# Four projections of a hybrid encoder block in seven block products of eight

## The chip, the core and the metric

The kernel runs on one core of a Trainium2 chip. The metric is the device time of one execution in microseconds (us): of three runs of the kernel before, 1034.06 to 1035.69 us, median 1035.56 us. The engines are named as in the profile: PE (TensorE, matrix products), DVE (VectorE), ACT (ScalarE), POOL (GpSimd) and SP (SyncE, which starts most DMAs).

## What is computed

One layer of a streaming encoder on 512 positions and 16 learned ones ahead of them, with model width 1024 and 2816 in the feed-forward. All is float32.

```python
u  = rmsnorm(h);  proj = u @ w_in                      # 1024 x 10256
y_conf = silu(layernorm(conv31(val * sigmoid(gate)))) @ w_conf_out
o      = chunk_gated_delta_rule(q, k, v, g, beta)      # 8 heads, sequential over chunks
y_dn   = (rmsnorm(o) * silu(z)) @ w_dn_out
h  = h + (g_conf * y_conf + g_dn * y_dn) @ w_out
up = conv3(rmsnorm(h) @ w_up)                          # 1024 x 5632
h  = h + (silu(up_gate) * up_val) @ w_down
out = rmsnorm(h)                                       # without the 16 learned positions
```

## The kernel before, in words

Activations lie transposed, features on the 128 partitions and positions along the row; a projection of 1024 features is eight tiles. Each weight tile (128 outputs x 1024 inputs, 512 KB) is one DMA into a buffer `wr` (three of them); `weights` (line 504) splits it into two parts in a rounded float32 form, `wh` by a cast on ACT and `wl` by a subtraction on DVE (two buffers of each). Activations are split in the same way by `split` (line 528): `oh`/`ol` for the delta rule's output, `ch`/`cl` for the convolution's, `mh`/`ml` for their gated sum, `hh`/`hl` for the second norm's input, `fh`/`fl` for the feed-forward.

`gemm` (line 515) makes one output tile: 8 input tiles, for each the three products low x high, high x high and high x low, each in two column halves of 258 to 260: 48 matmuls into one two-bank tile `p2` (two of them in PSUM). The eight output tiles of `w_dn_out` ('y'), of `w_conf_out` ('c', whose accumulators are named y too) and of `w_out` ('wo') follow the heads, then the 44 tiles of `w_up` ('up') and the 8 of `w_down` ('dn').

`up` (line 1207) multiplies the raw accumulator by the second norm's factor `r2` in two DVE instructions, so that PE can start on `w_up` before that factor is known; then three taps follow (ACT, and two DVE instructions `uy`), silu, the product with the other half, and the split into `fh`/`fl`.

In `grow` (line 893) the blocks of the heads' triangular inverses are put together by small matmuls (`gP`, `gX`); ahead of them, line 908 copies 32 blocks of 32x32x4 from `DU` into the tiles `Mn` (named mn) on ACT.

The order on each engine is made at build time: `Plan.order` (line 318) lists the instructions by priority, with prices of its own and offsets (`BIAS`, `LNP`, `UP` and others) by part of the program. On the chip each engine then works its list off in that fixed order, waiting at each instruction until what it needs is there.

```python
for i, (k, w, a) in enumerate(runs):
    for b, (c0, c1, *at) in enumerate(ranges):
        p0 = at[0] if at else 0
        PE.matmul(acc[:, b, p0:p0 + c1 - c0], lhsT=w[:, k * P:(k + 1) * P], rhs=a[k0 + k][:, c0:c1], ...)
```

Of the kernel before, what the change touches and what calls it, by code (L numbers as in the profile page):

```python
# [19 lines left out]
P = 128  # L20
# [16 lines left out]
ROW = T + PAD  # L37

# [104 lines left out]
RATE = 0.4453  # L143
# [37 lines left out]
GATES = [[12], [13], [15], [9], [0, 2], [], [7, 14, 8], [10, 1, 5, 3, 4, 6, 11]]  # L181

# [45 lines left out]
class Plan:  # L228
# [10 lines left out]
    def at(self, by, late=True):  # L239
# [3 lines left out]
        self.prio, self.late = self.prio + by, was or late and by > 0  # L243
# [3 lines left out]
    def add(self, eng, fn, a, k):  # L247
# [38 lines left out]
        o.tail = 950 + (2800 if fn == "dma_start" and o.lat > 700 and self.run(k) <= P else 0)  # L286
# [8 lines left out]
    def price(self, eng, fn, a, k, out):  # L295
# [10 lines left out]
        if fn == "dma_start":  # L306
            return 475, int(np.prod(out.shape)) * 4 / 290.0 * (1 if self.run(k) >= P else 2)
# [10 lines left out]
    def order(self):  # L318
# [70 lines left out]
        while len(out) < len(ops):  # L389
# [72 lines left out]
def record(A, out):  # L462
# [52 lines left out]
    def gemm(acc, ws, ah, al, ranges, k0=0, kn=None, first=True, last=True):  # L515
# [275 lines left out]
    def decays(h):  # L791
# [54 lines left out]

    ivt = {}
# [503 lines left out]
```

## Time and profile before

| | us |
|---|---|
| median of three runs | 1035.56 |
| the profiled execution | 1031.66 |
| its span, first to last instruction | 1029.9 |
| PE busy | 1015.1 |
| DVE busy | 717.1 |
| ACT busy | 473.6 |
| POOL busy | 9.4 |

The profile is one execution; its span leaves out some 1.8 us around it, and the execution itself is 3.9 us under the median. An engine's busy time is the time in which at least one of its instructions runs; idle time of an engine that nothing waits for costs nothing. Granted clock (PEclk) 1.00 is TensorE's upper level, 2.4 GHz.

### The profile page before, as it was taken

To read this page: it belongs to the slowest core of one execution; us is meant where nothing else is said; L and a number is where in the kernel's file an instruction comes from. 1 tells how busy PE (TensorE), PEld (TensorE's weight loads), DVE (VectorE), ACT (ScalarE), POOL (GpSimd) and SP (SyncE) were. 2 spreads that over 40 slices of the span, in tenths; PEclk is the share of its full clock that TensorE was granted. 3 is DMA by queue.
4 is the path that set the end of the run, shared out by engine and by line. 5 is a ranking of instruction groups with operands and counts; after the bars stand their busy time and mean duration, and the time that the engine had idled before them with its cause. 6 is when DMAs were issued, how large, how long until landed. Compare 5 with 4: busy or idle time off the path is not lost.

```text
span 1029.9 us, 20012 instructions
## 1 busy us (share of the span) xinstructions
PE 1015.1 (99%) x8430; PEld 973.8 (95%) x8430; DVE 717.1 (70%) x1237; ACT 473.6 (46%) x844; POOL 9.4 (1%) x45
## 2 busy tenths in 40 slices
PE   9998999999999999999999999999999999999996
PEld 7998999998999999999999999999999999988886
DVE  5987999999999999443565555666676767622334
ACT  6777713468545545444373334544434443422222
POOL 0000000000000000000000000000000000000000
PEclk9999999998999999999999999999999999999999
DMA  6243423241212133123214333222232222233332
GB/s 229 76 115 82 128 90 114 83 103 64 73 63 82 53 114 115 62 73 114 93 43 154 128 109 100 85 83 100 86 99 88 86 99 87 93 93 92 97 92 82
DMA packets 44042, 98.40 MB, mean 96 GB/s; under 512 B 12720, under 2 KB 19248, under 8 KB 43952
## 3 DMA queue, kind: packets, MB, share of 16 engines
q1 hardware_dynamic: 43952, 97.12, 29.5%
q8 instruction: 66, 1.08, 0.4%
q14 instruction: 24, 0.20, 0.1%
HBM read 93.89 MB, written 3.21 MB: 94 GB/s over the span
## 4 chain that ended last, share of the span: by engine, by line
PE 93%; DVE 4%; ACT 1%; DMA 1%; issue 0%; SPq 0%; DVEq 0%; ACTq 0%
PE up L459 25%; PE dn L459 12%; PE ga L459 9%; PE y L459 9%; PE q L459 5%; PE v L459 5%; PE z L459 5%; PE wo L459 5%; PE cv L459 4%; PE cg L459 4%; PE o L459 2%; DVE cv L459 1%; PE k L459 1%; PE rs L459 1%; PE S L459 1%; PE qk L459 1%
## 5 line engine op out<-in xcount | busy, mean ns | idle before, releaser
L459 DVE TENSOR_TENSOR wl<-wr,wh 128x1024 fp32r<-128x1024 f32 x157 | 189.2, 1206 | 154.3 <-PE dn L459 59.8
L459 ACT CAST wh<-wr 128x1024 fp32r<-128x1024 f32 x157 | 162.2, 1035 | 257.1 <-PE dn L459 58.2
L459 DVE SCALAR_TENSOR_TENSOR ca<-c,par,ca 128x516 f32<-128x516 f32 (+12 forms) x240 | 176.7, 745 | 3.7 <-ACT ca L459 1.0
L459 PE MATMUL up<-hl,wh 128*128 128x258 f32 x704 | 141.5, 282 | 0.0
L459 PE MATMUL up<-hh,wh 128*128 128x258 f32 x704 | 141.5, 282 | 0.0
L459 PEld LDWEIGHTS up<-hh,wh 128*128 128x128 f32 x704 | 109.2, 190 | 0.2 <-issue 0.2
L459 PEld LDWEIGHTS up<-hl,wh 128*128 128x128 f32 x704 | 108.7, 189 | 0.0
L459 PE MATMUL up<-hh,wl 128*128 128x258 f32 x704 | 92.3, 284 | 0.0
L459 PEld LDWEIGHTS up<-hh,wl 128*128 128x128 f32 x704 | 88.2, 190 | 0.0
L459 PE MATMUL dn<-fh,wh 128*128 128x512 f32 (+1 forms) x198 | 71.6, 370 | 0.0
L459 PE MATMUL dn<-fl,wh 128*128 128x512 f32 (+1 forms) x198 | 71.6, 370 | 0.0
L459 DVE SCALAR_TENSOR_TENSOR uy<-up,par,uy 128x512 f32<-128x512 f32 x88 | 65.9, 749 | 2.8 <-ACT uy L459 1.3
L459 DVE TENSOR_TENSOR up<-up,r 128x258 f32<-128x258 f32 x88 | 33.5, 420 | 47.4 <-PE up L459 44.6
L459 ACT ACTIVATE uy<-up,par 128x512 f32<-128x512 f32 x44 | 35.9, 817 | 55.8 <-DVE up L459 55.8
L459 PE MATMUL ga<-ul,wh 128*128 128x258 f32 (+1 forms) x256 | 58.0, 288 | 0.0
L459 PE MATMUL ga<-uh,wh 128*128 128x258 f32 (+1 forms) x256 | 57.2, 288 | 0.0
L459 DVE SCALAR_TENSOR_TENSOR cv<-ra,par,cv 128x528 f32<-128x528 f32 x69 | 51.7, 765 | 1.4 <-ACT cv L459 1.3
L459 PE MATMUL dn<-fh,wl 128*128 128x512 f32 (+1 forms) x198 | 45.4, 369 | 0.0
L459 PEld LDWEIGHTS dn<-fh,wh 128*128 128x128 f32 x198 | 37.2, 188 | 7.0
L459 PEld LDWEIGHTS dn<-fl,wh 128*128 128x128 f32 x198 | 37.2, 188 | 6.9
L459 PE MATMUL ga<-uh,wl 128*128 128x258 f32 (+1 forms) x256 | 43.1, 286 | 0.0
L459 PEld LDWEIGHTS ga<-ul,wh 128*128 128x128 f32 x256 | 42.2, 190 | 0.6 <-issue 0.4
(284 smaller groups left out, 2194.6 us busy)
## 6 DMA issues: line engine op xcount, KB each, us to landing
wr<-in_win SPq DMA_DIRECT2D x64, 512.0 KB, 3.4
wr<-in_wup SPq DMA_DIRECT2D x44, 512.0 KB, 3.4
wr<-in_wd SPq DMA_DIRECT2D x17, 512.0 KB, 3.5
wr<-in_wdn SPq DMA_DIRECT2D x8, 512.0 KB, 3.5
wr<-in_wco SPq DMA_DIRECT2D x8, 512.0 KB
wr<-in_wo SPq DMA_DIRECT2D x8, 512.0 KB, 3.4
wr<-in_wd SPq DMA_DIRECT2D x8, 384.0 KB, 3.5
x<-in_xT SPq DMA_DIRECT2D x8, 264.0 KB, 5.6
```

The lines of the kernel that those rows point to most:

```text
L459: getattr(engines[o.eng], o.fn)(*(get(x) for x in o.a), **{n: get(x) for n, x in o.k.items()})
```

## The change

Of the four projections of 'y', 'c', 'wo' and 'up', two output tiles (256 features) are made together, and two halves of the positions (258 each): a 2 x 2 block product, done in seven block products in the place of eight (`seven`). Each block product is 12 matmuls of 258 columns. The seven go by turns into two accumulators, each a one-bank tile of its own (`sx`, `sz`; four such tiles in all): three sums of weights and four of activations stand in for the operands, and partial results are read from an accumulator between two products that add up in it.

The sums of weights are made in DRAM, by accumulating DMAs that POOL starts (`presums`: five for a pair of tiles, 31 pairs; two pairs are under way at a time). The sums of activations are made by `factors` (four DVE instructions of 258 columns, four casts on ACT, four subtractions on DVE for a pair of tiles). `quarters` puts the results together in SBUF. The first three feed-forward tiles with their partners (`NPRE`, six of 44) stay as they were; for the rest the second norm's factor is multiplied into the activations ahead of the product. Residual tiles are written to DRAM and read back (`d_h`, `hr`). The copies of line 908 go from ACT to POOL. The planner's prices and offsets are new.

```diff
-BIAS = {'k3': -850, 'iv': -1500, 'd0': 150, ...
+BIAS = {'tp': 2330, 'h0': 400, 'h2': 240, ...
+NPRE = 3
+    def presums(src, n, hold):
+        r = [plan.tile("dram", "con", [P, 4, HD], F32, "ws") for _ in range(n)]
+        for m in range(n):
+          with plan.at(1):
+            h = {hold} | ({softs[-2]} if len(softs) > 1 else set())
+            plan.after = set(h)
+            G.dma_start(out=r[m][:, 0:2], in_=src[:, m, 0:3:2])
+            plan.after = set(h)
+            G.dma_start(out=r[m][:, 2:4], in_=src[:, m, 0:2])
+            G.dma_start(out=r[m][:, 1:3], in_=src[:, m, 3:4].broadcast_to([P, 2, HD]), accum_op=ALU.add)
+            G.dma_start(out=r[m][:, 0], in_=r[m][:, 1], accum_op=ALU.add)
+            G.dma_start(out=r[m][:, 3], in_=r[m][:, 0], accum_op=ALU.add)
+            softs.append(len(plan.ops) - 1)
+    def seven(src, m, sums, B, w, use):
+        X, Z = p1("sx")[:, :w], p1("sz")[:, :w]
+        tiles = (flat(src[:, m, 0:2]), flat(sums[m][:, 0:2]), flat(sums[m][:, 2:4]), src[:, m, 2])
+        for i, (b, to, first, what) in enumerate((('b11', X, True, 'p1'), ('b21', Z, True, 'c11b'),
+                                                  ('t2', X, False, 'u2'), ('t1', Z, True, 'c22b'),
+                                                  ('t3', X, False, 'u3'), ('b22', Z, False, 'c12b'),
+                                                  ('t4', X, False, 'c21'))):
+            if i % 2 == 0:
+                hi, lo = weights(tiles[i // 2], D if i < 6 else HD)
+            ...
+                PE.matmul(to, lhsT=x[:, c + k * P:c + (k + 1) * P], rhs=B[k][b][y], ...)
+            use(what, to)
+    def quarters(src, m, sums, B, w, n):
+            if what in ('p1', 'u2'):
+                S.copy(out=q(i, j), in_=acc)
+            elif what in ('c22b', 'c21'):
+                S.mul(out=q(i, j), in_=acc, mul=-1.0)
+            else:
+                V.tensor_tensor(out=q(i, j), in0=q(i, j), in1=acc, op=ALU.subtract if i else ALU.add)
...
-                S.copy(out=Mn[h][r, :, r], in_=D8(h)[r])
+                G.tensor_copy(out=Mn[h][r, :, r], in_=D8(h)[r])
...
+            g, v = quarters(A['wuq'], t - NPRE, wus, ub, 258, "up")
...
-            V.tensor_tensor(out=uv[:, b], in0=acc[:, b, :258], in1=r2v[b], op=ALU.mult)
```

The order on DVE in the feed-forward, before: two tiles (one pair). `wl` is the low part of a weight tile, the first `up` rows read accumulators, `uy` are taps, `fl` is the low part of the result.

```order
L459 TENSOR_TENSOR up_23_8660<-up_20_8588,r2_1_8033 128x258 x2
L459 TENSOR_TENSOR wl_101_8668<-wr_101_8484,wh_101_8634 128x1024
L459 SCALAR_TENSOR_TENSOR uy_11_8672<-up_23_8660,par_1_82,uy_11_8672 128x512 x2
L459 TENSOR_TENSOR up_25_8720<-up_22_8655,r2_1_8033 128x258 x2
L459 TENSOR_TENSOR wl_102_8729<-wr_102_8554,wh_102_8705 128x1024
L459 SCALAR_TENSOR_TENSOR uy_12_8732<-up_25_8720,par_1_82,uy_12_8732 128x512 x2
L459 TENSOR_TENSOR uy_11_8672<-uy_11_8672,uy_12_8732 128x512
L459 TENSOR_TENSOR fl_6_8782<-uy_11_8672,fh_6_8774 128x512
L459 TENSOR_TENSOR up_27_8790<-up_24_8718,r2_1_8033 128x258 x2
L459 TENSOR_TENSOR wl_103_8798<-wr_103_8614,wh_103_8764 128x1024
```

And one pair of it now; the rows with `sx` or `sz` read accumulators.

```order
L469 TENSOR_TENSOR up_36_10425<-up_36_10425,sx_24_10344 128x258
L469 TENSOR_TENSOR up_35_10375<-up_35_10375,sz_24_10365 128x258
L469 TENSOR_TENSOR wl_167_10469<-wr_167_10380,wh_167_10455 128x1024
L469 SCALAR_TENSOR_TENSOR uy_29_10467<-up_35_10375,par_1_69,uy_29_10467 128x512
L469 TENSOR_TENSOR wl_168_10493<-wr_168_10414,wh_168_10477 128x1024
L469 SCALAR_TENSOR_TENSOR uy_29_10467<-up_35_10375,par_1_69,uy_29_10467 128x512
L469 SCALAR_TENSOR_TENSOR uy_30_10497<-up_36_10425,par_1_69,uy_30_10497 128x512
L469 TENSOR_TENSOR up_37_10506<-up_37_10506,sz_25_10500 128x258
L469 TENSOR_TENSOR wl_169_10532<-wr_169_10442,wh_169_10515 128x1024
L469 SCALAR_TENSOR_TENSOR uy_30_10497<-up_36_10425,par_1_69,uy_30_10497 128x512
L469 TENSOR_TENSOR uy_29_10467<-uy_29_10467,uy_30_10497 128x512
L469 TENSOR_TENSOR wl_170_10564<-wr_170_10486,wh_170_10550 128x512
```

A pair has four rows of `wl` now, one of them half as wide, and three readings of 258 columns that lie between them; the multiplications by `r2` are gone.

The order on POOL before, from the last select of the decay masks to the clearings for the heads:

```order
L459 MEMSET ra_8_2494 128x4
L459 MEMSET ra_9_2575 128x4
L459 MEMSET LL_1_2901 32x8x32
L459 MEMSET LL_2_2908 32x8x32
L459 MEMSET LL_3_2914 32x8x32
L459 MEMSET LL_4_2983 32x8x32
L459 MEMSET ra_10_2783 128x4
L459 MEMSET ra_12_2898 128x4
L459 MEMSET ra_13_3580 128x4
```

And now, in the same part: the copies into `mn` stand among the DMAs that sum weights, and each accumulating DMA waits for the one before it on its tile (`ws`).

```order
L469 DMA ws_8_2866<-in_wco 128x1024
L469 MEMSET LL_1_3010 32x8x32
L469 DMA ws_7_2816<-in_wco 128x2x512
L469 MEMSET LL_2_3026 32x8x32
L469 COPY mn_1_1090<-DU_1_2894 32x4x32 x2
L469 COPY mn_2_1125<-DU_1_2894 32x4x32 x2
L469 COPY mn_3_1193<-DU_1_2894 32x4x32 x2
L469 COPY mn_1_1090<-DU_1_2894 32x4x32
L469 COPY mn_2_1125<-DU_1_2894 32x4x32
L469 COPY mn_3_1193<-DU_1_2894 32x4x32
L469 COPY mn_4_1273<-DU_1_2894 32x4x32 x3
L469 DMA ws_8_2866<-in_wco 128x2x512
```

Ahead of the first copy stand 35 of the 155 new DMAs, ahead of the last clearing for a head (`ra`) 88. What POOL had to do before, a list with hundreds of us of waiting in it, now stands behind those DMAs in one queue.

## Rows read from the trace of the kernel before

**Rows 1.** Page: the span; part 1, busy us of each engine.
```profile
span 1029.9 us, 20012 instructions
...
PE 1015.1 (99%) x8430; PEld 973.8 (95%) x8430; DVE 717.1 (70%) x1237; ACT 473.6 (46%) x844; POOL 9.4 (1%) x45
```

**Rows 2.** Busy time by stretch: us, PE, PEld, DVE, ACT, POOL (instructions), PEclk, DMA, GB/s.
```profile
495.80:546.00 50.20, 50.20 (x465) 49.77 (x465) 29.52 (x41) 27.28 (x40) 0.00 (x0) 1.00 0.26 85
...
674.50:894.70 220.20, 220.20 (x1837) 220.20 (x1837) 150.26 (x228) 91.62 (x116) 0.00 (x0) 1.00 0.28 92
...
0.00:495.80 495.80, 489.92 (x4429) 471.60 (x4430) 418.30 (x811) 270.50 (x583) 9.39 (x45) 0.99 0.30 96
...
495.80:894.70 398.90, 398.84 (x3362) 397.33 (x3362) 252.39 (x364) 166.49 (x215) 0.00 (x0) 1.00 0.29 97
```

**Rows 3.** The same view, a stretch in which DVE works without a break.
```profile
150.00:200.00 50.00, 50.00 (x410) 49.57 (x409) 49.89 (x109) 17.43 (x21) 1.28 (x6) 1.00 0.29 99
```

**Rows 4.** Groups of DVE: operation, shapes, count | busy us, mean ns of one.
```profile
L459 DVE TENSOR_TENSOR wl<-wr,wh 128x1024 fp32r<-128x1024 f32 x149 | 181.5, 1219 | 138.3 <-PE dn L459 48.0 <-ACT wh L459 42.0 <-PE ga L459 15.4
...
L459 DVE SCALAR_TENSOR_TENSOR uy<-up,par,uy 128x512 f32<-128x512 f32 x88 | 65.9, 749 | 2.8 <-ACT uy L459 1.3
...
L459 DVE TENSOR_TENSOR up<-up,r 128x258 f32<-128x258 f32 x88 | 33.5, 420 | 47.4 <-PE up L459 44.6 <-ACT r L459 2.8
...
L459 DVE TENSOR_TENSOR fl<-uy,fh 128x512 fp32r<-128x512 f32 x22 | 15.2, 692 | 29.0 <-ACT fh L459 29.0
...
L459 DVE SCALAR_TENSOR_TENSOR gt<-gt,y 128x516 f32<-128x516 f32 x16 | 11.0, 685 | 0.0
```

**Rows 5.** DVE in order of time, one pair of up tiles: start us, us, instruction.
```profile
693.57 0.75 DVE L459 TENSOR_TENSOR up<-up,r 128x258 f32<-128x258 f32 x2
...
694.24 1.21 DVE L459 TENSOR_TENSOR wl<-wr,wh 128x1024 fp32r<-128x1024 f32 x1
...
695.38 1.53 DVE L459 SCALAR_TENSOR_TENSOR uy<-up,par,uy 128x512 f32<-128x512 f32 x2
...
702.39 0.69 DVE L459 TENSOR_TENSOR uy<-uy,uy 128x512 f32<-128x512 f32 x1
```

**Rows 6.** Groups of ACT: operation, shapes, count | busy us, mean ns of one.
```profile
L459 ACT CAST wh<-wr 128x1024 fp32r<-128x1024 f32 x149 | 155.6, 1045 | 252.5 <-PE dn L459 53.7 <-PE up L459 45.3 <-PE y L459 34.3
...
L459 ACT COPY mn<-DU 32x128 f32<-32x128 f32 x32 | 9.1, 295 | 0.4
...
L459 ACT COPY r<-rc 128x258 f32<-128x258 f32 x2 | 0.7, 374 | 3.3 <-PE rc L459 3.3
```

**Rows 7.** PE in order of time: the first small products of the inverses.
```profile
225.41 1.20 PE L459 MATMUL gP<-LL,mn 32*32 32x32 f32 x64
```

**Rows 8.** POOL in order of time: selects, and a clearing of 32x256.
```profile
71.83 1.11 POOL L459 TENSOR_SCALAR_AFFINE_SELECT E<-E 128x512 f32<-128x512 f32 x1 [64.31 <-DMA E<-d_g]
...
75.11 0.63 POOL L459 TENSOR_SCALAR_AFFINE_SELECT E<-E 128x512 f32<-128x512 f32 x1 [2.17 <-DMA E<-d_g]
...
112.53 0.63 POOL L459 TENSOR_SCALAR_AFFINE_SELECT E<-E 128x512 f32<-128x512 f32 x1 [3.06 <-DMA E<-d_g]
...
199.42 0.30 POOL L459 MEMSET LL<- 32x256 f32 x1 [2.36 <-DVE cv L459]
```

**Rows 9.** DVE in order of time beside those selects.
```profile
72.36 1.13 DVE L459 SCALAR_TENSOR_TENSOR cv<-ra,par,cv 128x528 f32<-128x528 f32 x1
...
73.49 0.76 DVE L459 SCALAR_TENSOR_TENSOR cv<-k,par,cv 128x528 f32<-128x528 f32 x1
...
112.56 1.15 DVE L459 SCALAR_TENSOR_TENSOR ca<-c,par,ca 128x512 f32<-128x512 f32 x1
```

**Rows 10.** DMA: queue and total of the page, part 3; loads of part 6.
```profile
q1 hardware_dynamic: 43952, 97.12, 29.5%
...
HBM read 93.89 MB, written 3.21 MB: 94 GB/s over the span
...
wr<-in_wup SPq DMA_DIRECT2D x44, 512.0 KB, 3.4
```

More of the change, by code (lines that the diff above doesn't have):

```diff
@@ L242, in at @@
         was = self.late
-        self.prio, self.late = self.prio + by, was or late and by > 0
+        self.prio, self.late = self.prio + by, was or late
         yield
@@ new lines, in seven @@
+    def seven(src, m, sums, B, w, use):
+        X, Z = p1("sx")[:, :w], p1("sz")[:, :w]
+        flat = lambda v: v.rearrange("p b c -> p (b c)")
+        tiles = (flat(src[:, m, 0:2]), flat(sums[m][:, 0:2]), flat(sums[m][:, 2:4]), src[:, m, 2])
[4 more added lines that the diff above has]
+            if i % 2 == 0:
+                with plan.at("sw"):
+                    hi, lo = weights(tiles[i // 2], D if i < 6 else HD)
+            n, c = len(B), i % 2 * HD
+            runs = [(k, x, y) for part in PARTS for k in range(n) for x, y in ((lo, 0), (hi, 0), (hi, 1))[part]]
+            for j, (k, x, y) in enumerate(runs):
+                PE.matmul(to, lhsT=x[:, c + k * P:c + (k + 1) * P], rhs=B[k][b][y], start=first and j == 0, stop=j == len(runs) - 1,
+                          skip_group_check=not first)
+            use(what, to)
@@ L1132, in record, with gated @@
             gts[i] = call(gate, "t", i)
-    def gated(t, wsrc, ah, al):
-        acc = p2("y")
-        gemm(acc, weights(wsrc), ah, al, MIDR)
-        V.scalar_tensor_tensor(out=halves(t[:, :TW], HW), in0=halves(t[:, :TW], HW), scalar=1.0, in1=acc[:, :, MID],
-                               op0=ALU.add, op1=ALU.mult)
-        return t
-    chh, chl = [], []
+    def gated(m, wsrc, sums, B, ts):
+        for c, t in zip(quarters(wsrc, m, sums, B, HW, "yc"), ts):
+            V.scalar_tensor_tensor(out=t[:, :TW], in0=t[:, :TW], scalar=1.0, in1=c[:, :TW], op0=ALU.add, op1=ALU.mult)
+        return ts
+    for h in range(1, H, 2):
+        with plan.at(f"f{h}"):
+            ob.append(factors(zs[h - 1], zs[h], HW, "o", vals[-1]))
+    cb = []
     def layer_norm():
@@ L1200, in second_norm @@
+    d_h = [con([P, SEQ], "d_h", "dram") for _ in range(KT)]
+    for f in range(KT):
+        SY.dma_start(out=d_h[f], in_=hs[f][:, 4:TW])
+    r2v, ub = [], []
     def second_norm():
@@ L1224, in record, with ffn, ends, back @@
     fh, fl = [], []
[L1225 to L1226 removed]
+    def ffn(t):
+        if t < NPRE:
+            g, v = up(t), up(NPRE + t)
+        else:
+            g, v = quarters(A['wuq'], t - NPRE, wus, ub, 258, "up")
+        with plan.at("tp" if t < NPRE else "tq"):
+            ends(t, g, v)
+    def ends(t, g, v):
+        g = taps3(g, t)
         S.activation(out=g[:, :SEQ], in_=g[:, :SEQ], func=AF.Silu)
[L1228 removed]
+        v = taps3(v, FT + t)
         V.tensor_tensor(out=g[:, :SEQ], in0=g[:, :SEQ], in1=v[:, :SEQ], op=ALU.mult)
[L1230 removed]
+        if t < FT - 3:
+            a, b = split(g[:, :SEQ], SEQ, "f")
+        else:
+            hl = plan.tile("sb", "iv", [P, D], F32R, "fv")
+            a, b = hl[:, :SEQ], hl[:, SEQ:]
+            S.copy(out=a, in_=g[:, :SEQ])
+            V.tensor_tensor(out=b, in0=g[:, :SEQ], in1=a.bitcast(F32), op=ALU.subtract)
         fh.append(a)
         fl.append(b)
+    for t in range(FT):
+        call(ffn, "u", t)
     cuts = ((0, 8), (8, 8), (16, 6))
+    hr = []
+    def back(f):
+        o = bt(n="hr")
+        SY.dma_start(out=o[:, 4:TW], in_=d_h[f])
+        hr.append(o)
+        return o
     def wdown(f, i):
```

184 lines of the change are left out of this document (127 added, 57 removed).

## Prediction, made before the result was known

> **What bounds the kernel now.** I read the page first: PE is busy 1015.1 of 1029.9 us, DVE 717.1, ACT 473.6 [rows 1]. Then the busy time by stretch [rows 2]: from the first 'y' matmul (495.8) to the first 'dn' matmul (894.7), which is the stretch whose work the change cuts, PE has 398.84 of 398.90 us, at a granted clock of 1.00, the upper level. DVE has 252.39 there (63%) and ACT 166.49 (42%). So nothing but the number of matmuls sets this stretch, and a matmul taken out of it is time saved, as long as the other engines still keep up. In 674.5 to 894.7, 38 tiles of 'up' take 220.2 us: 38 x 48 = 1824 matmuls, 120.7 ns each. Ahead of 495.8 PE stands still 5.9 us in all.
>
> **What is taken out.** A pair of tiles costs 7 x 12 = 84 matmuls in the place of 96. There are 31 pairs (4 'y', 4 'c', 4 'wo', 19 'up'): 372 matmuls x 120.7 ns = 44.9 us. A product has the same width of 258 columns as before, so I keep the price of one. The stretch falls from 399 to about 2892 x 0.1207 = 349 us plus some 5 us of heads' and norms' matmuls in it, 354.
>
> **What DVE gets.** The sums of weights have to be split as well: 31 x 4 = 124 loads, a quarter of them half as wide, stand where 62 stood. I counted DVE's list from the first reading of a 'y' accumulator to the first of a 'dn' accumulator: 101 `wl` at 1219 ns, 31 half-wide ones at about 692, 192 instructions of 258 columns at about 420 (evictions and sums of activations; the multiplications by `r2`, 76 of 88, are gone), 88 taps at 749, 92 of 512 or 516 columns at 692, 16 gated at 685, and some 9 us of others [rows 4]: 123.1 + 21.5 + 80.6 + 65.9 + 63.7 + 11.0 + 9 = 375 us in 530 instructions. These durations overlap: two `up` rows and a `wl` start 0.67 and 1.14 us before the next, though they last 0.75 and 1.21 [rows 5], so about 0.08 us of each instruction lies under its successor. 375 - 530 x 0.08 = 332 us. The same sum for the kernel before (371 instructions, 276 us) gives 246 where the stretch shows 252 [rows 2], so I raise it by that 2.5%: 340 us. DVE then has 340 of 354 us, 96% where it had 63%. For one 'up' pair that is 13 instructions, 9.99 us of durations or 9.0 of occupancy against 84 x 0.1207 = 10.14 of PE. ACT gets 31 more full and 31 half casts of weights, 108 evictions at some 374 ns [rows 6] and the casts of the sums, some 110 us in all, and comes near 80%.
>
> **What that costs PE.** Three of the seven readings in a pair are DVE's, and the product after the next needs its accumulator back: PE's cover is one product, 1.45 us. A reading takes 0.34 us, and a `wl` started just ahead of it holds it 1.14 us. Before, PE never waited for DVE in this stretch, but there a whole tile of 48 matmuls, 5.8 us, lay between an accumulator's end and its buffer's reuse. Lower bound of the wait: nothing, since 340 is under 354 and in 150 to 200 us DVE ran 49.89 of 50 us without PE losing anything [rows 3] (there, however, most of DVE's work was the 31 taps of the convolution, for which no product waited). Upper bound: no overlap at all, 375 us, 21 us more than PE's 354, and with some handover losses 25. I take **10 us**, nearer to the lower end because the overlap is seen in the rows.
>
> **Heads and POOL.** The first `gP` waits for 16 copies into mn, which took ACT 295 ns each [rows 6]. On POOL a clearing of twice the width takes 0.30 us and a select of 512 columns 0.63 [rows 8]; 16 copies take 3 to 5 us alone. But a select beside a DVE instruction took 1.11 us, and the DVE instruction 1.13 in the place of 0.76 [rows 8, 9], so a copy may cost up to 0.8 us more, 13 us for 16, with DVE full of taps just there. PE waits in order at `gP`: 0 to 15 us for both halves of the heads, and I take **4**, since ACT is relieved of the same copies and runs them no more. The Trainium skill has this as a rule (SBUF — State Buffer, Who interferes with whom): a DVE instruction with two SBUF inputs and a GpSimd one that reads SBUF block each other, the later one until the first is done. The trace agrees (1.13 and 1.11 us); by the rule's full blocking the sum would carry the 13 us, by the undisturbed rows none.
> The rest of the new order I take at nothing: DVE's list up to the last head's last step is as long as before (397 us of occupancy in both), while 126 matmuls have moved from ahead of it to behind, where the longer chain from the last head through its sums to the first 'y' product needs cover (374 matmuls stand there, 255 before). Counted as above, DVE gets 23 us more ahead of 'y' (the layer norm and the first sums of activations), where it had 418 of 496 us [rows 2]. Writing the residuals out and back is 16 transfers of 258 KB beside a queue that is 29.5% busy [rows 10].
>
> **The sum.** 1031.7 - 44.9 + 10 + 4 = 1000.8 us for an execution like the profiled one; that one lay 3.9 us under the median of the three runs, so **1005 us** for the median.
>
> **Rivals.**
> *DVE sets the pace.* If the overlap goes where waits lie between (a reading waits for PE, `fl` for ACT's cast), the stretch takes DVE's 375 us and the handovers: 25 us in the place of 10, **1020 us**. For it: 96%, and a fixed order in which both engines wait for each other; against it: the rows of the full stretch [rows 3].
> *Weights come too late.* In 'y', 'c' and 'wo' 42 loads of 512 KB are used up in 122 us, one in 2.9 us, 181 GB/s; POOL's sums write 2.1 MB for a pair of tiles, about 124 GB/s at the pace below. Together 305 GB/s, where 29.5% busy moved 96 [rows 1, 10], so some 325 when all are busy. If the loads get half of that (163 GB/s), each is 0.3 us late, 13 us in all, and with reads of the accumulating DMAs counted twice that: **1020 to 1030 us**.
> *POOL's queue is late (slower).* POOL's list is one queue: 35 DMAs (7 pairs) lie between the last select (112.5 [rows 8]) and the copies, needed near 231 us (51 matmuls later than the 225.4 of [rows 7]); 88 (17.6 pairs) lie ahead of the last `ra`, needed near 415. Both leave 17 us for a pair of tiles. What one takes no row shows. From below: two pairs at a time move 4.2 MB in four dependent steps; at 325 GB/s 13 us, and four times the 1.8 us by which a 512 KB load (3.4 us to landing [rows 10]) exceeds its 1.6 at full rate: 20 us for two, 10 for one. From above: accumulating moves its bytes twice and the weights keep 30% of the engines: 17.4. At the upper end nothing much is late yet. At 20 us the last `ra` is 17.6 x 3 = 53 us late, and PE, waiting in order for the head behind it, with it: **about 1056 us**, slower than before. It decides from 17 + 31/17.6 = 18.8 us on.
> *The products aren't what limits*, so that the time stays: excluded nearly by [rows 2]; 3% for sums that come out even by chance.
>
> **Chances and range.** Forecast 0.60 (own range 992 to 1014); DVE sets the pace 0.15; weights late 0.10; POOL late 0.12, of which 0.02 stays faster; even 0.03. Faster by over 0.2% (about what a measurement of this kernel tells from no change): 0.60 + 0.15 + 0.10 + 0.02 = 0.87; same 0.03; slower 0.10. The range goes from no waits at all, 1035.6 - 44.9 = 991, to the late weights, 1028; it leaves out POOL's case and the even one.
>
> **What would show it.** In the profile after: PE busy near 970 us and some 12 to 16 us of idle between 'y' and 'dn' with DVE as the releaser (`yc`, `up`, `wl`), an 'up' pair every 10.2 to 10.6 us, DVE above 90% there. DVE setting the pace: a pair every 10.9 us and PE's waits nearly all on DVE. Late weights: DVE's and ACT's waits on loads, a landing well above 3.4 us in 'y' to 'wo' and none later. POOL late: PE idle ahead of `gP` or in the heads, with POOL as the releaser and its DMAs without a gap. The prediction is wrong if a matmul of 258 columns now costs more than 121 ns, if the clock falls below the upper level during the waits, or if the heads' part moves by more than 5 us.

## Result and the profile after

The changed kernel takes 1042.8 us (median of 8 runs, 1038.5 to 1047.2) where the kernel before takes 1035.4 on the same chip: a ratio of 1.0077, 95% interval 1.005 to 1.0104. It is slower by 0.8%; the forecast was 1005 us, the range 991 to 1028. The profiled execution took 1039.8 us, with a span of 1038.0. The ratios here and below leave out the slowest runs of two kernels whose runs lie far apart, e10 (1040 to 1061 us) and e13 (1027 to 1053 us).

The page of the changed kernel: span, part 1, the two queues that move data (part 3: packets, MB, share of 16 engines), the total, and four kinds of transfer of part 6 (KB each, median us to landing).

```profile
span 1038.0 us, 20271 instructions
...
PE 988.9 (95%) x8058; PEld 940.4 (91%) x8058; DVE 819.6 (79%) x1444; ACT 560.3 (54%) x1023; POOL 154.7 (15%) x232
...
q1 hardware_dynamic: 55184, 125.70, 37.0%
q0 software_dynamic: 26288, 65.02, 32.6%
...
HBM read 185.38 MB, written 70.32 MB: 246 GB/s over the span
...
wr<-in_win SPq DMA_DIRECT2D x64, 512.0 KB, 6.9
...
ws<-in_wuq POOLq DMA_DIRECT2D x57, 512.0 KB, 8.6
ws<-ws POOLq DMA_DIRECT2D x62, 256.0 KB, 6.7
...
wr<-in_wd SPq DMA_DIRECT2D x17, 512.0 KB, 3.4
```

The products were saved (372 matmuls fewer), and PE works 26 us less than before [rows 1], yet it stands still 49 us where it stood 15. The new queue, q0, is POOL's: it carries the sums of weights. It moved 65.02 MB in 32.6% of 1038 us of all 16 engines, 192 GB/s; SP's queue moved 125.7 MB in 37.0%, 327 GB/s. While sums run a load of 512 KB lands after 6.9 us; in `wd`, when they are over, after 3.4, as before [rows 10]. These medians stand for the few loads whose landing the trace dates (7 of the 64 of `in_win`, 3.2 to 8.1 us).

The busy time of the changed kernel by stage: PE, PEld, DVE, ACT, POOL in us (instructions), granted clock, DMA share, GB/s. The stretches are: up to the first small product of the inverses; up to the first 'y' product; 'y'; 'c'; 'wo'; the six tiles of 'up' in eight products; the 19 pairs in seven; 'dn'.

```profile
0.00:232.30 232.30, 227.20 (x1844) 217.28 (x1844) 211.62 (x496) 124.25 (x270) 45.17 (x81) 1.00 0.68 181
232.30:505.60 273.30, 268.76 (x2665) 259.21 (x2665) 227.30 (x363) 155.22 (x317) 74.94 (x111) 0.99 0.85 194
505.60:556.70 51.10, 44.81 (x338) 43.36 (x337) 36.75 (x62) 25.14 (x44) 11.51 (x13) 0.93 0.91 243
556.70:613.10 56.40, 44.04 (x338) 42.19 (x336) 38.56 (x62) 25.04 (x42) 12.71 (x16) 0.97 0.97 251
613.10:672.20 59.10, 47.67 (x337) 44.99 (x337) 41.36 (x72) 25.38 (x36) 9.55 (x11) 0.88 0.97 272
672.20:708.90 36.70, 36.60 (x305) 36.00 (x306) 32.39 (x64) 22.42 (x33) 0.84 (x1) 1.00 0.46 136
708.90:903.20 194.30, 193.47 (x1599) 192.32 (x1597) 180.86 (x264) 142.48 (x231) 0.00 (x0) 1.00 0.57 179
903.20:1038.00 134.80, 126.34 (x644) 105.06 (x642) 50.79 (x69) 40.39 (x53) 0.00 (x0) 0.97 0.35 109
```

The 19 pairs of 'up' are what the prediction wanted: 194.3 us, 10.2 a pair, with DVE busy 93% and no sum running (POOL 0.00). The loss is in the three rows from 505.6 to 672.2: 336 matmuls of 'y', of 'c' and of 'wo' are worth 40.6 us each, and took 51.1, 56.4 and 59.1, at DMA shares of 0.91 to 0.97 and with the clock partly at its lower level. DVE is busy there only 70% of the time.

What was waited for from 505.6 to 672.2 in the changed kernel (us, times, longest), for the weights' cast on ACT and for PE; and the same view for SP's queue.

```profile
PEld sx L469 <- ACT wh L469: 21.2, 11, 3.9
...
PE sx L469 <- ACT wh L469: 17.4, 8, 3.7
...
ACT wh L469 <- DMA wr<-in_wco: 12.1, 6, 4.5
...
ACT wh L469 <- DMA wr<-in_wdn: 10.0, 3, 5.7
ACT wh L469 <- DMA wr<-in_wo: 9.5, 3, 4.3
ACT wh L469 <- DMA wr<-ws: 8.2, 5, 4.1
```
```profile
SPq L469 <- DVE wl L469: 81.9, 32, 9.4
```

PE waits for ACT's cast, the cast for the load. SP's queue, though, waits for DVE's `wl`: for the instruction that reads a buffer last. The chain of waits shows one turn of that ring (start us, us, what):

```profile
571.76 1.14 DVE wl L469
572.92 9.16 DMA wr<-in_wco
582.17 1.05 ACT wh L469
583.27 1.23 PE sx L469 x8
```

A `wl` ends, its buffer is free, the load is issued and takes 9.16 us, then comes the cast. Seven other loads of these three projections in this chain took 7.16 to 10.43. A chain picks the late ones; in all, ACT waited for 17 of the 48 loads, 39.8 us, and these 17 took 5.7 to 10.5 us, 7.7 in the mean, from issue to cast.

### The profile page after: what moved, and what is told of

Read it like the earlier page. It is cut to its first block, busy times and chain, and to the rows that moved or that the text cites. A ratio compares the mean times of both kernels' runs of the same rounds, so it can differ in the third digit from the quotient of the medians.

```text
span 1038.0 us, 20271 instructions
## 1 busy us (share of the span) xinstructions
PE 988.9 (95%) x8058; PEld 940.4 (91%) x8058; DVE 819.6 (79%) x1444; ACT 560.3 (54%) x1023; POOL 154.7 (15%) x232
## 3 DMA queue, kind: packets, MB, share of 16 engines
q0 software_dynamic: 26288, 65.02, 32.6%
## 4 chain that ended last, share of the span: by engine, by line
PE 70%; DVE 13%; DMA 11%; ACT 4%; issue 2%; SPq 0%; ACTq 0%; DVEq 0%
PE sx L469 13%; PE dn L469 12%; PE sz L469 9%; PE ga L469 5%; PE v L469 4%; PE z L469 4%; PE k L469 4%; DVE wl L469 4%; DVE ca L469 3%; PE q L469 3%; PE up L469 3%; DMA wr<-in_wco 2%; DMA orb<-d_r 2%; DMA wr<-in_wo 2%; ACT wh L469 2%
## 5 line engine op out<-in xcount | busy, mean ns | idle before, releaser
L469 ACT CAST wh<-wr 128x1024 fp32r<-128x1024 f32 (+2 forms) x219 | 213.8, 978 | 251.0 <-PE dn L469 52.3
L469 DVE TENSOR_TENSOR wl<-wr,wh 128x1024 fp32r<-128x1024 f32 (+2 forms) x219 | 248.0, 1135 | 122.0 <-PE dn L469 60.7
L469 DVE SCALAR_TENSOR_TENSOR ca<-c,par,ca 128x516 f32<-128x516 f32 (+11 forms) x240 | 176.9, 742 | 3.3 <-ACT ca L469 0.6
L469 POOL DMA_DIRECT2D ws<-ws x62 | 57.9, 942 | 172.3 <-DMA ws<-ws 75.7
L469 POOL DMA_DIRECT2D ws<-in_wuq x57 | 49.0, 866 | 162.7 <-DMA ws<-in_wuq 79.9
L469 PE MATMUL sx<-nh,wh 128*128 128x258 f32 x228 | 59.8, 286 | 0.7 <-ACT wh L469 0.5
L469 PE MATMUL sz<-nh,wh 128*128 128x258 f32 x228 | 59.3, 282 | 0.0
L469 PE MATMUL sz<-nl,wh 128*128 128x258 f32 x228 | 59.2, 283 | 0.0
L469 PE MATMUL sx<-nl,wh 128*128 128x258 f32 x228 | 59.2, 283 | 0.0
L469 PEld LDWEIGHTS sx<-nh,wh 128*128 128x128 f32 x228 | 43.3, 190 | 1.5 <-ACT wh L469 0.7
```

The lines of the kernel that those rows point to most:

```text
L469: getattr(engines[o.eng], o.fn)(*(get(x) for x in o.a), **{n: get(x) for n, x in o.k.items()})
```

## Experiments

Sixteen kernels. e1, e2, e3, e9 and e13 compute other numbers, as the expectations say: they price a part and are of no other use; the rest are complete. The table gives for each the median of its runs, the ratio to the kernel before on the same chip with its interval, and from its profile the start of the first 'y' product, the length of 'y' to 'wo' and that of the 19 pairs of 'up', in us.

| run | median | ratio | 'y' begins | 'y' to 'wo' | 'up' pairs |
|---|---|---|---|---|---|
| before | 1035.4 | | 495.8 | 143.9 | |
| changed | 1042.8 | 1.005 to 1.010 | 505.6 | 166.6 | 194.3 |
| e1 no 'up' sums | 1012.5 | 0.977 to 0.983 | 502.0 | 141.7 | 194.2 |
| e2 no sums | 1005.6 | 0.970 to 0.974 | 496.9 | 141.3 | 194.1 |
| e3 plain copies | 1017.7 | 0.980 to 0.990 | 498.5 | 153.0 | 194.2 |
| e4 copies on ACT | 1044.6 | 1.006 to 1.013 | 508.6 | 167.2 | 194.2 |
| e5 pause | 1081.7 | 1.045 to 1.048 | 507.7 | 141.3 | 259.4 |
| e5b pause, one token | 1052.5 | 1.016 to 1.021 | 504.9 | 142.0 | 234.8 |
| e7 'up' alone | 1029.8 | 0.995 to 0.997 | 516.8 | 144.0 | 197.3 |
| e7b same, POOL free | 1024.4 | 0.990 to 0.995 | 509.0 | 143.9 | 198.2 |
| e8 mixers alone | 1039.4 | 1.004 to 1.008 | 508.0 | 138.9 | |
| e9 seam cut | 1003.3 | 0.969 to 0.973 | 495.8 | 139.5 | 194.4 |
| e10 POOL free | 1047.2 | 1.006 to 1.013 | 513.4 | 168.1 | 195.3 |
| e11 'up' alone, later sums | 1018.9 | 0.983 to 0.988 | 509.0 | 144.0 | 197.6 |
| e12 four buffers | 1023.6 | 0.986 to 0.992 | 507.5 | 147.4 | 193.9 |
| e13 sums unread | 1041.9 | 0.998 to 1.005 | 505.3 | 167.4 | 194.2 |
| e15 four buffers, later sums | 1023.8 | 0.988 to 0.994 | 497.2 | 144.7 | 208.6 |
| e16 as e11, ACT copies | 1019.1 | 0.983 to 0.988 | 505.9 | 144.1 | 197.0 |

### Is it the sums? (e1, e2, e13)

The edit of e1, and of e2 with every sum in the place of those of 'up': the sums are not issued, the two loads of a pair that read them read two blocks of the weights.

```
     SY.dma_start(out=w[:, :n], in_=src)
+    if alt is not None:
+        plan.ops[-1].alt = {'in_': alt}
...
     softs.append(len(plan.ops) - 1)
+    if src is A['wuq']:
+        for o in plan.ops[-5:]:
+            o.skip = True
```

> Leaves out the 19 pairs' worth of weight sums for 'up' (95 of POOL's 155 DMAs); the loads that read them read the same size straight from the weights, so these products are of other numbers. All else stands in the order of the changed kernel; the twelve pairs of sums for 'y', 'c' and 'wo' stay. Theory 1, the sums take the DMA engines from the loads of 'y' to 'wo': at 18.5 us a pair the twelve end near 104.9 + 12 x 18.5 = 327 us, 'y' to 'wo' falls from 166.7 us to between 122 and 130, granted clock 1.00 there, total 998 to 1006 us. Theory 2, DVE and ACT set the pace from 'y' to 'wo': their work is the same, so the time stays at 1041 to 1045. Theory 3, the new layout of the weights makes each load slow: the stretch stays above 155 us and the time above 1030.

> Leaves out all weight sums (all 155 DMAs on POOL's queue); the loads that read them read the same size straight from the weights, so these products are of other numbers. Order as in the changed kernel. Theory 1 (the sums take the DMA engines from the loads): 'y' to 'wo' 122 to 130 us, and the heads ahead of it, too, are back at the pace of before: first 'y' product near 500.6 us instead of 505.5, landing of a load of in_win near 3.4 us instead of 6.9, total 992 to 1000 us. If the heads' loss comes from POOL's copies into mn and not from the loads, 'y' still begins near 505 and the total equals that of the run without the 'up' sums. Theories 2 and 3 (DVE's pace, or the layout): 1030 to 1045 us.

Theory 1 holds, but the stretch from 'y' to 'wo' came down to 141 us, not to the 122 to 130 that it gave: 25 us came back, 19 more than the matmuls are still there, and the totals lie 6 us above their ranges. Theories 2 and 3 fall: DVE's and ACT's work and the layout are the same in all three kernels. The stages of e2 (heads in two rows, 'y', 'c', 'wo', 'up'), and its landing:

```profile
0.00:231.10 231.10, 227.16 (x1846) 217.12 (x1846) 212.18 (x496) 124.43 (x270) 22.69 (x60) 1.00 0.37 116
231.10:496.90 265.80, 265.33 (x2666) 256.59 (x2666) 228.00 (x364) 156.05 (x317) 4.23 (x18) 1.00 0.23 78
496.90:538.60 41.70, 41.19 (x338) 40.57 (x338) 35.94 (x61) 25.16 (x44) 0.00 (x0) 1.00 0.54 167
538.60:584.50 45.90, 41.62 (x339) 40.58 (x337) 37.84 (x62) 24.84 (x42) 0.00 (x0) 1.00 0.60 193
584.50:638.20 53.70, 46.41 (x337) 44.03 (x338) 41.07 (x71) 25.86 (x37) 0.00 (x0) 0.90 0.58 183
...
675.00:869.10 194.10, 193.26 (x1598) 192.21 (x1597) 180.80 (x264) 142.20 (x231) 0.00 (x0) 1.00 0.56 179
```
```profile
wr<-in_win SPq DMA_DIRECT2D x64, 512.0 KB, 3.3
```

Of the 33.9 us between the two spans 8.7 lie ahead of 'y' and 25.3 from 'y' to 'wo'; the rest is even to 0.2. So the sums cost 34 us of the profiled execution (37 of the medians). ACT's waits for loads are gone in e2; its only one from 'y' to 'wo':

```profile
ACT wh L472 <- DMA wr<-in_wco: 0.2, 1, 0.2
```

In e13 the sums run, and no load reads them; `alt` is the only edit:

```
-    hi, lo = weights(tiles[i // 2], D if i < 6 else HD)
+    hi, lo = weights(tiles[i // 2], D if i < 6 else HD, flat(src[:, m, i // 2 - 1:i // 2 + 1]) if i in (2, 4) and True else None)
```

> All sums run as in the changed kernel, but no load reads them: the loads read the same size from the weights themselves (numbers are wrong for it). It separates loads that wait for an unfinished sum from loads that are slow beside the sums. If no load waits for a sum and the engines' time is the cause: 'y' to 'wo' 160 to 172 us, total 1036 to 1046. If loads wait for sums that are late, and hold SP's queue: 'y' to 'wo' near 141, total 1006 to 1016.

Its median is that of the changed kernel, though its runs lie far apart, and the stretch takes 167.4 us. So it isn't the waiting for unfinished sums that costs: the loads are slow beside the sums.

### What makes a sum dear? (e3)

```
     o = self.ops[i]
+    o.k.pop('accum_op', None)
```

> Every DMA of the sums stays, but none accumulates: three of five become plain copies of the same size (so the summed weights are of other numbers). If accumulating is what makes a byte of the sums dear (the target is read too): a pair of sums takes about 11 us instead of 18.5, they end near 450 us, ahead of 'y', and the time falls to about 1000 to 1010 us. If it is the path that POOL's DMAs take from DRAM to DRAM, whatever they do there: a pair takes 16 to 19 us, and the time stays at 1035 to 1043 us.

In between: the last pair's last DMA is issued at 563.3 us instead of 677.3, some 14.8 us a pair instead of 18.5, and 'y' still has sums beside it (53.1 us), 'c' only at its start, 'wo' no more. Plain copies thus delay a load as much: in this 'y' ACT waited for 6 loads, 13.0 us, and four of the five loads in its chain of waits took 7.1 to 7.9 us. What accumulating adds is that the sums last into 'c' and 'wo'. Queue q0 of e3:

```profile
q0 software_dynamic: 18352, 65.02, 21.9%
```

The same bytes take 21.9% of 1017.5 us: 292 GB/s instead of 192. Half of the bytes are accumulated in the changed kernel. At 292 GB/s the plain half takes 111 us of the 338; the accumulated half takes the other 227: an estimate of 143 GB/s, half the rate of a copy. The packets in the trace show the same. The accumulated bytes go in packets of 2 KB, plain ones in packets of 4 KB (26288 packets against 18352), and in the changed kernel one of 2 KB takes 0.236 us, one of 4 KB 0.205. The Trainium skill states (DMA: Bandwidth & Descriptors, Rules for kernel authors) that an accumulating DMA reads its destination and writes it later. The trace counts no bytes for that reading (65.02 MB in both kernels), so no run here shows that it is the reason. A pair's pace fell less, by a fifth; what else holds it isn't separated.

### By what do they hold the loads up? (e12)

```
-    bufs=SLOTS[t.tag], name=nm)
+    bufs=SLOTS[t.tag] + (t.tag == 'wr'), name=nm)
```

> The changed kernel, complete, in the same order, with four buffers in the place of three for loads of weights (wr). Tells whether the loads of 'y' to 'wo' are late by latency or by the engines' throughput. Latency: 42 loads in three buffers, each buffer taken for about 9 us of landing and 2.9 of use, give 42 x 11.9 / 3 = 167 us, which is what the stretch took; with four 42 x 11.9 / 4 = 125, and so 130 to 145 us there, total 1010 to 1025. Throughput (95% of the engines' time is taken there): a fourth load in flight makes all of them land later, the stretch stays above 155 us, total 1033 to 1044.

Its 'y', 'c' and 'wo':

```profile
507.50:550.80 43.30, 41.71 (x338) 40.67 (x337) 36.06 (x61) 25.20 (x44) 9.55 (x13) 1.00 0.96 253
550.80:598.90 48.10, 42.02 (x338) 40.75 (x336) 37.95 (x61) 24.75 (x42) 8.21 (x10) 1.00 0.99 283
598.90:654.90 56.00, 46.86 (x336) 44.02 (x336) 41.59 (x72) 25.30 (x36) 11.48 (x13) 0.91 0.99 282
```

The sums run as before (POOL's column), the DMA share is even higher, and still the stretch falls from 166.6 to 147.4 us, 19.2 of the 25.3 that the sums cost there (2 us above the range that I gave). ACT now waits for 6 loads, 7.6 us in all, instead of 17 and 39.8; the largest of these waits:

```profile
ACT wh L469 <- DMA wr<-ws: 4.7, 4, 2.3
```

The engines were not out of throughput; the loads were out of time. An estimate with the chain's numbers: a load of some 8.3 us, cast 1.05 and `wl` 1.2 are 10.6 us for a buffer; 48 loads (a quarter of them half as wide) in three buffers make 48 x 10.6 / 3 = 170 us. With the 7.7 us of the 17 late loads it is 159; measured were 166.6. At a landing of 3.4 us it is 5.7 a buffer and 91 us, under the 122 of the matmuls. The point from which the loads decide is 122 / 48 x 3 - 2.3 = 5.3 us to landing, and all 17 loads that ACT waited for took longer. With four buffers it is 7.9.

### Does it only matter where loads follow closely? (e5, e5b, e11, e15)

In e5 the last ten pairs of sums are held behind a copy on POOL that waits for the last 'wo' result; e5b has that copy once only.

```
+    if i > self.tok[2] and o.eng == 'PE' and held:
+        engines['POOL'].tensor_copy(out=self.tok[0].make(), in_=self.tok[1].make())
+        for p in held:
+            engines['POOL'].dma_start(...)
```

> The changed kernel, complete, with one thing moved: the sums of the last 10 'up' pairs stand on POOL's queue behind one tiny copy that waits for the last 'wo' result, so that the first 21 pairs' sums end near 104.9 + 21 x 18.5 = 493 us and none runs from the first 'y' product to the last of 'wo'. Theory 1 (the sums take the DMA engines from the loads there): 'y' to 'wo' takes 141 to 145 us, as in the run without the 'up' sums, in the place of 166.6; 'y' still begins near 505; in 'up', where the engines were busy 57% of the time, ten pairs of sums at 10.9 us of all engines are 109 of 231 us and fill them to about 100%, so 'up' may lose 0 to 15 us: total 1015 to 1032 us. Theory 2 (DVE and ACT set the pace of 'y' to 'wo', and leaving out sums helped in some other way): the stretch stays above 160 us, total 1038 or more.

> The kernel with the pause again, complete; the first version also held ACT for 38 us in 'up' (the copy that waits for the last 'wo' result stood a second time at the end of POOL's queue, and a buffer could not be reused until then); here it stands once. 'y' to 'wo' 141 us as there. In that run the stretch from 686 to 800 us, with sums beside 'up', had PE busy 97 of 114 us. If the loss only moves with the sums: 'up' takes 210 to 225 us in the place of 194.3, total 1033 to 1045 us. If 'up' can carry them (its loads come to 57% of the engines): 194 to 200 us, total 1014 to 1022.

In both 'y' to 'wo' comes down to that of e2 at once (141.3 and 142.0 us). But 'up' pays: 234.8 us in e5b, 40 more, worse than I had said. Its loads follow each other as closely (four in 10.2 us, 2.5 us each as in 'y' to 'wo'), and ten pairs of sums from 645 us on, near 21 us each, lie beside 'up' until about 855. e5 takes 29 us more than e5b for another reason: a second copy of that kind stood at the end of POOL's queue and held a buffer that ACT needed; ACT waited 37.9 us for it.

In e11 'up' alone is in seven products (below), and its sums begin behind POOL's copies into mn, the clearings of `ra` being on DVE:

```
+    wus = presums(A['wuq'], FT - NPRE, copied[-1])
```

> 'up' alone in seven products, complete; its 19 pairs of sums begin only behind POOL's copies into mn (near 245 us) instead of at 112 us, and the clearings of ra stand on DVE. 19 x 18.5 us from 245 on end near 597 us, most of the last third beside 'y' and 'c', which in eight products load 512 KB for 5.8 us of matmuls (25 to 45% of the engines without sums). If the loads beside the sums only hurt where a load lasts PE less than it takes to land: 'y' begins at 496 to 502 us, 'y' to 'up' stays at 144 to 150, total 1006 to 1013 us. If the sums cost PE their share of the engines wherever they run: 'y' to 'up' 155 us or more, total above 1018.

'y' in e11, with sums beside it, and in e7b, without:

```profile
509.00:559.50 50.50, 50.50 (x467) 50.00 (x466) 31.59 (x45) 27.63 (x41) 11.99 (x15) 1.00 0.88 182
```
```profile
509.00:559.30 50.30, 50.30 (x466) 49.85 (x465) 29.57 (x41) 27.33 (x40) 0.00 (x0) 1.00 0.23 85
```

A DMA share of 0.88 or 0.23, and 'y' takes the same: with a load for 5.8 us of matmuls (48 of them) the ring has 17 us for a buffer. So from 'y' on sums cost where a load is used up in 2.5 us and nothing where it lasts 5.8. At 1018.9 us e11 is the fastest complete kernel here, with e16; that it stayed above my 1013 lies in the heads (below).

In e15 the changed kernel has four load buffers, the sums start at 232 us, and the clearings of `ra` are on DVE.

```
+    wds, wcs, wos = (presums(A[n], KT // 2, copied[-1]) for n in ('wdn', 'wco', 'wo'))
+    wus = presums(A['wuq'], FT - NPRE, copied[-1])
```

> The changed kernel, complete, with four load buffers and, besides, all 31 pairs of sums only behind POOL's copies into mn (near 245 us) instead of at 112 us, the clearings of ra on DVE. The heads' loss (first 'y' product at 507.5 us with four buffers, 496.9 without sums) is still unexplained: if it comes from the sums between 112 and 245 us, 'y' begins at 497 to 502; if from the sums after 245 us or from POOL's copies, at 504 to 510. 31 x 18.5 us from 245 on end near 818 us, ahead of the last pair's need at about 880. If four buffers carry the loads beside the sums (147 us for 'y' to 'wo' as before), 'up' stays below 200 us: total 1012 to 1026. If 'up' needs more than four: 'up' 205 us or more, total above 1030.

Its second stretch of the heads, and 'up':

```profile
227.70:497.20 269.50, 269.42 (x2702) 260.75 (x2702) 231.08 (x382) 157.38 (x318) 65.40 (x84) 1.00 0.83 197
...
678.70:887.30 208.60, 199.38 (x1599) 193.70 (x1598) 182.32 (x264) 142.47 (x231) 29.02 (x36) 1.00 0.87 241
```

'y' begins at 497.2 us as without sums, so what the heads lose comes from the sums ahead of that point, not from those beside the later heads (POOL 65 us there, DMA 0.83); the fourth buffer alone (e12) and POOL's small work alone (e10) leave the loss. What it gains there over e12, 10 us, 'up' gives back, 15 us, since the last pairs' sums now lie beside it: with four buffers a third of what e5b lost. For 'up', then, four buffers are not enough.

### The parts by themselves (e7, e8)

e7 has 'y', 'c' and 'wo' and their weights as before, and the order's numbers of before; e8 has all of 'up' in eight products. From e7, and from e8:

```
-    wds, wcs, wos = (presums(A[n], KT // 2, masks[-1]) for n in ('wdn', 'wco', 'wo'))
...
+    ydn = [call(lambda f: gated(gts[KT + f], A['wdn'][f], oh, ol), "y", f) for f in range(KT)]
```
```
-NPRE = 3
+NPRE = FT
```

> One part of the change alone, complete: only 'up' in seven products (19 pairs, as in the changed kernel); 'y', 'c' and 'wo' in eight products as before, with one load for 5.8 us of products and without sums; the heads in the order of before, with the copies into mn on POOL. 19 pairs of sums at 18.5 us end near 456 us, ahead of 'y'. Theory 1: 'up' gains 19 x 12 x 0.1207 = 27.5 us less 1.5 of waits, 'y' to 'wo' is as before, the heads lose 5 to 9 us to the sums as in the changed kernel: 1012 to 1018 us. If the sums delay the heads much more where they stand on the order of before (rival: POOL's queue late): above 1025. If nearly all of the gain belonged to the mixers: 1030 or more.

> The other part alone, complete: 'y', 'c' and 'wo' in seven products with their 12 sums, all of 'up' in eight products as before. The sums end near 327 us, so no sum runs from 'y' on. By the run without 'up' sums, where 'y' to 'wo' took 141.7 us with no sum beside it, the 144 matmuls saved (17.4 us) go to the waits at the seams between c, wo and up, and the heads lose about 5 us: total within 4 us of before, 1033 to 1040. If the products saved are time saved (17.4 less some 3 us of waits, less 5 in the heads): 1024 to 1028.

e8: what the mixers save is gone without any sum beside them. 'y' to 'wo' takes 138.9 us, before 143.9, for 144 matmuls (17.4 us) fewer. And of these 5 us some 4 are no gain: 80 small matmuls of the layer norm, which lay in 'y' before, lie ahead of it in the new order. The heads lose 12 in this profile, these 4 among them; it is of the slowest of five runs, 4 us above the median. So the gain of the change is 'up' alone.

e7 loses 21 us in the heads. There the rival *POOL's queue is late* shows itself. What was waited for in e7's heads, and the place in POOL's order of time:

```profile
PE kS L469 <- DVE S L469: 12.2, 1, 12.2
DVE cv L469 <- POOL ra L469: 12.1, 2, 10.5
```
```profile
253.59 0.84 POOL L469 DMA_DIRECT2D ws<-ws  x1 [5.40 <-DMA ws<-in_wuq]
255.32 0.82 POOL L469 DMA_DIRECT2D ws<-ws  x1 [0.90 <-DMA ws<-ws]
255.84 0.45 POOL L469 MEMSET ra<- 128x4 f32 x2
```

A clearing of four columns stands behind two accumulating DMAs, each waiting for the one ahead of it; DVE waits 10.5 us for it, and PE 12.2 for DVE.

### POOL's small work (e4, e7b, e10, e16)

e4 puts the copies into mn back on ACT; e7b (on e7) and e10 (on the changed kernel) do that and put the clearings of `ra` and `LL` on DVE; e16 is e11 with the copies on ACT.

```
+    if o.eng == 'POOL' and o.fn == 'tensor_copy':
+        o.eng, o.fn = 'ACT', 'copy'
+    if o.eng == 'POOL' and o.fn == 'memset' and o.tiles[0].name in ('ra', 'LL'):
+        o.eng = 'DVE'
```

> The 32 copies into mn go back from POOL to ACT, at the same place of the order; the sums stay as they are. If the copies on POOL are what holds the first gP product (240.4 us where 231 was expected): gP comes 5 to 9 us earlier, and the total falls by 2 to 8 us, to 1035 to 1041. If the heads' loss is the loads' (theory 1): gP stays within 2 us and the total within 2 us of 1042.8.

> The kernel with 'up' alone in seven products, complete, with POOL's small work in the heads taken off its queue: the copies into mn on ACT, the clearings of ra and LL on DVE, each at its place of the order, so that POOL carries only sums from 112 us on. In the run before this one PE waited 12.2 us in the heads for a chain that began with a clearing of ra queued on POOL behind sums (10.5 us), and 'y' began at 516.8 us. If POOL's queue is the cause: 'y' begins at 497 to 503, total 1010 to 1017 us. If the loads late beside the sums are the cause: 'y' stays after 510 and the total at 1024 to 1030.

> The changed kernel, complete, with POOL's small work in the heads taken off its queue in the same way. In it 'y' began at 505.6 us, and at 496.9 without any sums. If that loss of 8.7 us is POOL's queue: 'y' begins near 498 and the total falls to 1032 to 1036 us. If it is the loads beside the sums: 'y' stays at 503 to 507. 'y' to 'wo' stays at 160 to 170 us in either case, since sums run there as before: a total of 1038 to 1043 then.

> 'up' alone in seven products with the sums behind 225 us, complete, as in the run that began them at 245, but with the copies into mn on ACT, at their place of the order, and the first sum behind one tiny POOL copy that waits for the same data. In the three runs of 'up' alone 'y' began at 509.0 to 516.8 us (495.8 before), and from 229 to 265 us the granted clock was 0.50 to 0.60, where before it was 0.73 to 1.00. If the copies on POOL delay the small products there and so let the clock fall: 'y' begins at 497 to 502 us, total 1007 to 1012. If the clock falls whatever engine copies (in the second of the three ACT did, beside sums): 'y' stays at 507 to 511, total 1016 to 1023.

In the changed kernel POOL's small work costs nothing: e4 and e10 are not faster (1044.6 and 1047.2 us, the second above both of its ranges), the first small product comes at 234 us in both as against 232.3 (the 240.4 in my expectation is wrong), and 'y' begins later. In e7b PE's wait for `ra` is gone, 'y' begins 7.8 us earlier, and the time falls by 5. But 13 us of the heads stay lost in the profiles of e7b and e11 and 10 in that of e16, whoever copies. The one of e11 is its slowest run, 5.9 us above its median. An estimate from the medians, with what each profile saves from 'y' on taken off, gives 12 us in e7b, whose sums begin at 109 us, 4 in e11 (235) and 7 in e16 (218): a later start helps here as well, as in e15. What the three profiles share is a low clock at about 245 us; the window of 10 us in e11 and in the kernel before:

```profile
245.00:255.00 10.00, 9.49 (x57) 9.05 (x57) 6.26 (x12) 4.67 (x10) 2.96 (x3) 0.50 0.44 64
```
```profile
245.00:255.00 10.00, 10.00 (x108) 9.40 (x107) 9.28 (x17) 8.31 (x24) 0.00 (x0) 0.92 0.02 9
```

PE was at 1.2 GHz there in e11 (0.50), after waits ahead of it (8.50 of 10 us busy from 235 to 245), and a `gP` matmul of 64 rows took 313 ns instead of 220. What starts it in these orders is open.

### What is left without sums (e9)

```
     V.scalar_tensor_tensor(out=t[:, :TW], in0=t[:, :TW], scalar=1.0, in1=c[:, :TW], op0=ALU.add, op1=ALU.mult)
+    if wsrc is A['wco']:
+        plan.ops[-1].skip = True
...
     V.tensor_tensor(out=y[:, :TW], in0=y[:, :TW], in1=ydn[2 * m + i][:, :TW], op=ALU.add)
+    plan.ops[-1].skip = True
```

> Leaves out all weight sums as in the run without them and, besides, the 16 DVE instructions that take the results of 'c' into the gates (times c, plus y), so that the factors of 'wo' no longer wait for the products of 'c'; numbers are wrong for both reasons. It prices the chain of DVE and ACT between the last 'c' product and the first of 'wo'. If that chain is what 'c' and 'wo' lose without any sums (45.9 and 53.7 us, where 336 matmuls take 40.6): the two together fall from 99.6 to 83 to 90 us, granted clock 1.00 there, and the total from 1005.6 to 991 to 997 us. If they lose it to the loads of weights (one in 2.9 us): they stay above 95 us and the total at 1001 or more (the 11 us of DVE's own work are gone in either case).

'c' and 'wo' fall only from 99.6 to 97.8 us. These numbers are those of the second reading, loads of weights, but its cause isn't in the rows: ACT's cast waited for PE there, and for no load. ACT's largest wait in 'c' and 'wo' of e9:

```profile
ACT wh L472 <- PE sz L472: 18.0, 10, 4.7
```

So neither reading is shown. Cutting the dependency did not take the wait away, since ACT and DVE kept the order of their lists. e2's PE at the seam (start us, us; in brackets the idle time before and its releaser):

```profile
584.49 0.39 PE L472 MATMUL sx<-mh,wh 128*128 128x258 f32 x1 [1.93 <-ACT wh L472]
...
590.35 0.58 PE L472 MATMUL sx<-ml,wh 128*128 128x258 f32 x1 [0.97 <-DVE ml L472]
...
593.03 1.23 PE L472 MATMUL sx<-mh,wl 128*128 128x258 f32 x4 [1.50 <-DVE wl L472]
```

Between the last 'c' and the steady part of 'wo' PE waits in turn for the cast of the weights, the splits of the factors and `wl`, and 0.42 to 0.58 us for a matmul show the lower clock. Which of these would have to move is open.

## Why the prediction was wrong

- **What bounds the kernel, and what is taken out**: right. 1596 matmuls of the 19 pairs are 192.6 us at 120.7 ns, and took 194.1 to 194.3.
- **DVE beside PE**: 10 us; without sums PE lost 1.5 us in the pairs of 'up', where I had feared it at 93% of DVE, and 19.6 from 'y' to 'wo' (141.3 - 121.7), where I had not looked. The price was half of what it should be, and in the wrong place: 'c' and 'wo', at the seams, where e2's PE waits in turn for casts, splits and `wl`; the cause there isn't shown (e9). The overlap held (DVE's 340 us came out at 328 in e2); *DVE sets the pace* did not occur.
- **Heads and POOL**: the copies cost nothing (e4), not 4. Without sums 'y' begins at 496.9 us, where the sum implies 500 (1000.8 less 364 for the stretch and 137 behind it).
- **The sum**: without the sums of weights the kernel takes 1005.6 us and the forecast was 1005. That is partly luck: 'y' to 'dn' took 372 us where I had 364, and the heads 3 less than I had, although the 4 us of the layer norm's small matmuls had moved into them.
- **The step that failed**: the sum has no term for the loads beside the weight sums. I had them only as the rival *Weights come too late*, with 13 us (up to 26) and 0.10. From 'y' to 'wo' it came true with 25, and with the heads, where the way is open, the sums cost 34. I compared rates (305 of 325 GB/s) and took the lateness as a load's small deficit. Both terms were wrong. The sums' bytes move at 192 GB/s, not 325, as the accumulated half moves at half a copy's rate. And what decides is not the engines' throughput but the time to landing in a ring of three buffers: [rows 10] gives 3.4 us, and only with no second queue. Worked out as a ring (48 loads, three buffers, 2.3 us of cast and split) the limit is 5.3 us, and a landing that doubles beside the sums is over it. I had all the numbers of that but the landing beside the sums, whose bound from above I didn't set.
- ***POOL's queue is late***: the place was right, the price near my upper end: 18.5 us a pair against 10 to 17.4, just under the 18.8 that I gave as its turning point. In the changed kernel it did not decide (e10); with the order of before it cost 8 us of the heads (e7 against e7b), and e7 was not slower for it. The sign came from another rival. (Its time is 1005 + 53 = 1058 us by my own terms, not 1056.)
- **The signs I named**: "a landing well above 3.4 us in 'y' to 'wo' and none later" is what the trace shows, though it shows it in the heads as well, and the clock's fall during the waits, which I named as what would make it wrong, added to it.

Open: which transfer or wait of the heads the sums delay in their first 130 us (8.7 us; for loads of weights ACT waited there 6.6 us in the changed kernel and 1.9 in e2); what starts the low clock in e7, e7b, e11 and e16; and whether a load's landing doubles by its share of the 16 engines or by something in the DRAM, which no run separates.

## What to carry to other kernels

When work is traded for transfers, price the loads as a ring: (landing + what reads the buffer) / buffers against the time that a load's products last; and take the landing with the new traffic beside it, not from the quiet trace. An accumulating DRAM transfer is no copy: here it cost twice. And a saving has to be looked for stage by stage: here 'up' gave 26 us, and the three short projections gave 3 to 5 of 17, and 4 of that was work that had only moved ahead of them.

## Not expected of the hardware

- Beside POOL's sums a 512 KB load took 6.9 us instead of 3.3 (medians of the 7 dated loads of `in_win`, changed kernel and e2), though SP's queue has the higher rate of the two (327 against 192 GB/s) and the engines were 68 to 85% busy.
- Accumulating from DRAM to DRAM ran at an estimated 143 GB/s of all 16 engines, plain copies on the same queue at 292.
- With a DMA share of 0.99 'c' took 48.1 us, at 0.97 and one buffer less 56.4: the busy share of the DMA engines doesn't tell whether loads are late.
